# HGRN2 factors of both directions in one tile, the queries read in place, and the second pair of heads projected earlier

## The chip, the core and the metric

The kernel runs on one core of a Trainium2 chip. The metric is the device time of one execution in microseconds (us), as the median of several runs. The engines are named as in the profile: PE (TensorE, matrix products; its weight loads are PEld), DVE (VectorE), ACT (ScalarE), POOL (GpSimd) and SP, whose queue starts nearly all transfers. Each engine works its instructions in order and waits where a semaphore tells it to.

## What is computed

One inference step of a backbone of two layers on 384 tokens (128 of a prompt, 256 of a sample) of width 1024. The first layer's mixer joins windowed attention (mixer A) with a bidirectional HGRN2 of four heads of 128 channels (mixer B), both fed by one input projection. The change is in mixer B alone:

```
qb = silu(q) * dk**-0.5                       # per head, 384 tokens x 128 channels
f  = lb + (1 - lb) * sigmoid(z)               # one gate per direction; log f is the decay, k = 1 - f
cum = cumsum(log f)                           # in chunks
attn[t, s] = sum_k qb[t, k] * exp(cum[t, k] - cum[s, k]) * k[s, k]   for s <= t
o = attn @ v + (qb * exp(cum)) @ state_at_chunk_start
# the backward direction is the same on the flipped sequence; o_f + flip(o_b)
```

The sum over the channels holds a decay that depends on both tokens, so it isn't one matrix product. It is split by halves: for a query t and a key s that lie in the two halves of one block, the decay is a product of one factor up to the border and one from the border.

## The kernel before

The four heads are done as two pairs (pair 0 and pair 1). For a pair, a tile holds 2 heads x 384 tokens = 768 columns, with the 128 channels on the partitions. `hg_proj` projects the queries (`proj_fm` with `ev_q`) and the gates of both directions (`ev_f`): of the gates come f, in two tiles of tag "qf", and 1 - f, in two tiles of tag "X", through a sigmoid on ACT and three steps on DVE each. Every `proj_fm` takes two weight tiles of 512 KB through `wload`: a transfer on SP's queue, a cast on ACT (L122) and a subtraction on DVE (L123); three matmuls of 384 columns for each product, since a float32 is split into a high and a low part.

`hg_levels` then goes through a diagonal step and seven levels. At level lv a block has two halves of m = 2**lv tokens. There are four tiles of factors: forward and backward queries Fq, Bq, and forward and backward keys Fk, Bk. A level does this: four copies on ACT (L890 to L893) put the second halves of Fq and the first halves of Bq into one tile Qc, and the first halves of Fk and the second halves of Bk into one tile Kc. Four multiplies on DVE (L900, 384 columns each) bring the factors to the next level, two small ones (L907, L908) the products over blocks. PE computes six 128 x 128 score matmuls of Kc and Qc ("hs", L872), four and then two, both into the one PSUM bank "lv"; DVE merges each part under a mask into the attention matrix "at" (L911), so the second part waits for the first merge. The two multiplies of the keys and the two of the queries may run as soon as the copies have read the factors.

`hg_out` transposes the keys ("tk", L933), updates the states ("up", L938), multiplies the attention with the values ("ho"), normalises, gates and transposes back ("ty", L971) for the output projection ("o", L127 to L129).

The order of each engine is fixed when the program is built, by a scheduler that simulates the program and takes instructions by priority. Priority follows the order in which the code is written, shifted by `ahead(part)` and the number for that part in the table AHEAD (L30); "lv0" is -30 and "lv1" 0. In the code the order is: context loads `a_ctx`, the key and value projection and the query projection of mixer A, the levels of pair 0, the projection of pair 1, the projections of values ("ib") and output gates ("gb"), the levels of pair 1, the attention, then the two outputs. Beside all that, PE also works off pieces of later conditioning vectors ("ada_acc", L203, "ada_t", L221), which wait for transfers of their own ("ar", L232).

Of the kernel before, what the change touches and what calls it, by code (L numbers as in the profile page):

```python
# [9 lines left out]
F32 = mybir.dt.float32  # L10
# [31 lines left out]
def tile_backbone_step(ctx, tc, I, O):  # L42
# [775 lines left out]
    def mixer_ab():  # L818
# [4 lines left out]
        M = Slots(es, {"one": (1, 0), "pr": (4, 768), "pt": (6, 512), "qS": (2, 1536), "qf": (3, 768),  # L823
                       "X": (8, 768), "at": (2, 768), "vB": (2, 768), "kq": (3, 768), "t2": (5, 512),
# [4 lines left out]
        def hg_tiles():  # L829
            return M.tile("qf", F32), [M.tile("X", F32) for _ in range(4)], [M.tile("qf", F32) for _ in range(2)]  # L830
# [9 lines left out]
        def ev_f(pr, d, X, f):  # L840
            def ev(j, acc):
                c = slice(4 * d + 2 * pr + j, 4 * d + 2 * pr + j + 1)
                sl = slice(j * NTOK, (j + 1) * NTOK)
                sg = M.sm.tile([P, NTOK], F32, tag="sg", name="sg")
                nc.scalar.activation(sg, acc, AF.Sigmoid)
                nc.vector.tensor_scalar(out=X[2 + d][:, sl], in0=sg, scalar1=C["nomlb"][:, c],
                                        scalar2=C["omlb"][:, c], op0=ALU.mult, op1=ALU.add)
                nc.vector.tensor_scalar(out=f[d][:, sl], in0=sg, scalar1=C["omlb"][:, c], scalar2=C["lb"][:, c],
                                        op0=ALU.mult, op1=ALU.add)
                nc.vector.tensor_scalar(out=f[d][:, sl], in0=f[d][:, sl], scalar1=1e-30, scalar2=None, op0=ALU.max)  # L850
            return ev

        def hg_proj(pr):
            q, X, f = hg_tiles()
            proj_fm(w, 768 + 256 * pr, ev_q(q))
            proj_fm(w, 1792 + 256 * pr, ev_f(pr, 0, X, f))
            proj_fm(w, 2304 + 256 * pr, ev_f(pr, 1, X, f))
            return q, X, f


        def hg_levels(q, X, f, out):
            Fq, Bq, Fk, Bk = X
            nc.vector.tensor_tensor(out=Fq, in0=q, in1=f[0], op=ALU.mult)
            nc.vector.tensor_tensor(out=Bq, in0=q, in1=f[1], op=ALU.mult)
            AT = M.tile("at", F32).rearrange("p (b t) -> p b t", b=6)

            def scores(Kc, Qc, take):
                for b0, nb in ((0, 4), (4, 2)):
                    pp = lvt("hs").rearrange("p (b t) -> p b t", b=4)
                    for b in range(nb):  # L870
                        bs = slice((b0 + b) * P, (b0 + b + 1) * P)
                        nc.tensor.matmul(pp[:, b, :], Kc[:, bs], Qc[:, bs], start=True, stop=True)  # L872
                    take(pp[:, 0:nb, :], slice(b0, b0 + nb), nb)
# [7 lines left out]
            scores(Kc, q, diag)  # L881
            yield
            Bf, Bb = f
            for lv in range(7):
                m = 1 << lv
                G = 2 * NTOK // (2 * m)
                V = lambda a: a.rearrange("p (g h m) -> p g h m", h=2, m=m)
# [6 lines left out]
                w_ = max(1, m // 2)  # L894
                bf = Bf.rearrange("p (g h w) -> p g h w", h=2, w=w_)[:, :, :, 0]
                bb = Bb.rearrange("p (g h w) -> p g h w", h=2, w=w_)[:, :, :, 0]
                bc = lambda a: a.unsqueeze(2).to_broadcast([P, G, m])
# [3 lines left out]
                if lv == 0:  # L901
                    nB = M.sm.tile([P, 2, NTOK], F32, tag="nB", bufs=1, name="nB")
                    Bf, Bb = nB[:, 0, :], nB[:, 1, :]
                    nf, nb_ = Bf, Bb
                else:
                    nf, nb_ = bf[:, :, 0], bb[:, :, 0]
                nc.vector.tensor_tensor(out=nf, in0=bf[:, :, 0], in1=bf[:, :, 1], op=ALU.mult)  # L907
                nc.vector.tensor_tensor(out=nb_, in0=bb[:, :, 0], in1=bb[:, :, 1], op=ALU.mult)  # L908
# [8 lines left out]
            for d, B in enumerate((Bf, Bb)):  # L917
                nc.vector.tensor_copy(out=eb[:, d, :], in_=B.rearrange("p (g w) -> p g w", w=64)[:, :, 0])
            out.extend((AT, eb))

        def hg_out(pr, X, AT, eb, vB):
            Fq, Bq, Fk, Bk = X
# [85 lines left out]
        st0 = hg_tiles()  # L1008
# [131 lines left out]
        lv0, lv1 = [], []  # L1140
        a_ctx()
# [4 lines left out]
        st1 = hg_proj(1)  # L1146
# [382 lines left out]
```

## Time and profile before

| | |
|---|---|
| median of 3 runs | 1097.33 us (1095.86 to 1098.22) |
| the profiled execution | 1095.94 us |
| its span in the trace | 1094.1 us |
| PE busy | 1036.0 us, 95% of the span |
| DVE, ACT, POOL busy | 660.6, 440.8, 120.0 us |
| mean granted clock of PE | 0.981 |

The profiled execution is one of its own beside the three runs. Its span runs from the first to the last instruction in the trace; what lies around it is the other 1.84 us. A busy share is a mean over stages with different limits, so the prediction reads single stretches. [...] Instruction durations of engines that work in a pipeline overlap a little, so that a row's start and the next row's start tell more than its length. Float32 matmuls show as two records each.

### The profile page before, as it was taken

To read this page: it belongs to the slowest core of one execution; us is meant where nothing else is said; L and a number is where in the kernel's file an instruction comes from. 1 tells how busy PE (TensorE), PEld (TensorE's weight loads), DVE (VectorE), ACT (ScalarE), POOL (GpSimd) and SP (SyncE) were. 2 spreads that over 40 slices of the span, in tenths; PEclk is the share of its full clock that TensorE was granted. 3 is DMA by queue.
4 is the path that set the end of the run, shared out by engine and by line. 5 is a ranking of instruction groups with operands and counts; after the bars stand their busy time and mean duration, and the time that the engine had idled before them with its cause. 6 is when DMAs were issued, how large, how long until landed. Compare 5 with 4: busy or idle time off the path is not lost. (4 is left out here: it accounts for less than half of the span.)

```text
span 1094.1 us, 15881 instructions
## 1 busy us (share of the span) xinstructions
PE 1036.0 (95%) x6105; PEld 870.7 (80%) x6105; DVE 660.6 (60%) x1140; ACT 440.8 (40%) x804; POOL 120.0 (11%) x166
## 2 busy tenths in 40 slices
PE   5999999987999999999999998979899999999996
PEld 4788767555889999897778786666589999998885
DVE  2575855686598458458236875765489464443237
ACT  2365645363253323232223547545254333332231
POOL 0021201101110000000000343213130000000004
PEclk8999999997999999999999999989999999999998
DMA  9874243484047776766655431144126555543431
GB/s 305 258 222 124 86 142 123 140 275 164 23 150 219 249 221 219 232 210 214 237 190 159 152 108 45 35 150 165 47 79 194 151 172 153 159 135 116 135 116 58
DMA packets 114354, 173.13 MB, mean 158 GB/s; under 512 B 9419, under 2 KB 82150, under 8 KB 114278
## 3 DMA queue, kind: packets, MB, share of 16 engines
q1 hardware_dynamic: 113526, 171.78, 50.0%
q8 instruction: 48, 0.79, 0.3%
q10 hardware_dynamic: 752, 0.34, 0.1%
q14 instruction: 28, 0.23, 0.1%
HBM read 167.84 MB, written 4.24 MB: 157 GB/s over the span
## 5 line engine op out<-in xcount | busy, mean ns | idle before, releaser
L123 DVE TENSOR_TENSOR wl<-wr,wh 128x1024 fp32r<-128x1024 f32 (+4 forms) x200 | 235.7, 1182 | 234.9 <-ACT wh L122 232.3
L122 ACT ACTIVATE wh<-wr 128x1024 fp32r<-128x1024 f32 (+4 forms) x200 | 202.4, 1015 | 347.3 <-PE pf L128 124.0
L127 PE MATMUL pf<-hH,wh 128*128 128x384 f32 x688 | 232.7, 338 | 0.0
L129 PE MATMUL pf<-hH,wl 128*128 128x384 f32 x688 | 232.7, 338 | 0.0
L128 PE MATMUL pf<-hL,wh 128*128 128x384 f32 x688 | 232.6, 338 | 0.0
L129 PEld LDWEIGHTS pf<-hH,wl 128*128 128x128 f32 x688 | 129.4, 188 | 3.1 <-issue 3.1
L128 PEld LDWEIGHTS pf<-hL,wh 128*128 128x128 f32 x688 | 129.4, 188 | 2.7 <-issue 2.6
L127 PEld LDWEIGHTS pf<-hH,wh 128*128 128x128 f32 x688 | 129.4, 188 | 2.3 <-issue 2.2
L128 PE MATMUL o<-wl,aH 128*128 128x512 f32 (+1 forms) x280 | 101.2, 361 | 0.7 <-DVE wl L123 0.7
L127 PE MATMUL o<-wh,aH 128*128 128x512 f32 (+1 forms) x280 | 101.3, 362 | 0.4 <-DVE a L1175 0.4
L129 PE MATMUL o<-wh,aL 128*128 128x512 f32 (+1 forms) x280 | 101.0, 361 | 0.0
L129 PE MATMUL pj<-wh,hL 128*128 128x512 f32 (+3 forms) x240 | 89.0, 371 | 2.0 <-POOL hL L344 1.8
L127 PE MATMUL pj<-wh,hH 128*128 128x512 f32 (+3 forms) x240 | 89.2, 377 | 0.3 <-ACT vA L1106 0.2
L261 DVE SCALAR_TENSOR_TENSOR part<-ar,cT,part 128x512 f32<-128x512 f32 x112 | 80.2, 744 | 15.3 <-DMA ar<-in_w_ada 15.2
L128 PE MATMUL pj<-wl,hH 128*128 128x512 f32 (+3 forms) x240 | 89.0, 371 | 0.0
L110 POOL TENSOR_TENSOR ve<-ve,nhalf 128x1 f32<-128x1 f32 x12 | 7.0, 583 | 617.7 <-DVE ve L530 336.1
L127 PEld LDWEIGHTS o<-wh,aH 128*128 128x128 f32 x280 | 52.9, 189 | 10.2 <-issue 1.4
L128 PEld LDWEIGHTS o<-wl,aH 128*128 128x128 f32 x280 | 52.9, 189 | 9.0 <-DVE wl L123 1.0
L129 PEld LDWEIGHTS o<-wh,aL 128*128 128x128 f32 x280 | 52.8, 188 | 9.2 <-issue 1.2
L129 PEld LDWEIGHTS pj<-wh,hL 128*128 128x128 f32 x240 | 45.1, 188 | 12.2 <-POOL hL L344 2.7
L127 PEld LDWEIGHTS pj<-wh,hH 128*128 128x128 f32 x240 | 44.8, 188 | 10.4 <-issue 2.7
L128 PEld LDWEIGHTS pj<-wl,hH 128*128 128x128 f32 x240 | 45.1, 188 | 8.6 <-issue 1.4
(318 smaller groups left out, 1542.7 us busy)
## 6 DMA issues: line engine op xcount, KB each, us to landing
ar<-in_w_ada SPq DMA_DIRECT2D x80, 512.0 KB
wr<-in_w_ffn_down SPq DMA_DIRECT2D x44, 512.0 KB
wr<-in_w_ffn_gate SPq DMA_DIRECT2D x40, 512.0 KB
wr<-in_w_ffn_up SPq DMA_DIRECT2D x40, 512.0 KB
wr<-in_w_in_ab SPq DMA_DIRECT2D x18, 512.0 KB
ar<-in_w_ada SPq DMA_DIRECT2D x32, 256.0 KB
wr<-in_w_out SPq DMA_DIRECT2D x16, 512.0 KB
wr<-in_w_in_ab SPq DMA_DIRECT2D x16, 256.0 KB
```

The costliest lines, as they stand in the source:

```text
L110: nc.gpsimd.tensor_tensor(out=out, in0=v, in1=nhalf[:, :n], op=ALU.pow)
L122: nc.scalar.activation(hi, raw, AF.Copy)
L123: nc.vector.tensor_tensor(out=lo, in0=raw, in1=hi.bitcast(F32), op=ALU.subtract)
L127: nc.tensor.matmul(out, lh, rh, start=start, stop=False)
L128: nc.tensor.matmul(out, lh, rl, start=False, stop=False)
L129: nc.tensor.matmul(out, ll, rh, start=False, stop=stop)
L261: nc.vector.scalar_tensor_tensor(out=dst, in0=raw[:, j], scalar=sc, in1=dst, op0=ALU.mult, op1=ALU.add)
```

## The change

The factors of both directions come to lie in one tile, keys in one and queries in another: K holds forward and backward keys, Q backward and forward queries, each in 2 x 768 columns and some spare ones ("X" is now 4 tiles of 1664 columns). A view `mixed(X, m)` steps from the first half of a block in one direction to the second half in the other, so that one view names all columns that a level needs. f of both directions is one tile of 1536 columns too.

With this a level has one copy on ACT instead of four: the keys, 768 columns, into a contiguous tile. The queries aren't copied; PE reads them through the view, in runs of m neighbouring columns, as the moving operand. On DVE one multiply of 768 columns takes the place of the two for the keys (L916 in the changed kernel), the two for the queries stay (L918, L919), and the products over blocks are one instruction (L925). In the code, the multiplies of the queries now stand behind the level's scores, which read what they overwrite.

The projection of pair 1 moves ahead of the context loads and of mixer A's projections. Its f takes a tile of tag "qS". The levels themselves stand where they stood.

```diff
@@ mixer_ab @@
-        M = Slots(es, {"one": (1, 0), "pr": (4, 768), "pt": (6, 512), "qS": (2, 1536), "qf": (3, 768),
-                       "X": (8, 768), "at": (2, 768), "vB": (2, 768), "kq": (3, 768), "t2": (5, 512),
+        M = Slots(es, {"one": (1, 0), "pr": (4, 768), "pt": (6, 512), "qS": (2, 1536), "f": (1, 1536),
+                       "X": (4, 1664), "at": (2, 768), "vB": (2, 768), "kq": (3, 768), "t2": (5, 512),
                        "gB": (1, 1536)})
+        N2 = 2 * NTOK
+        def half(X, i):
+            return X[:, i * N2:(i + 1) * N2]
+        def mixed(X, m):
+            v = X[:, 0:2 * (N2 + m)].rearrange("p (h r) -> p h r", h=2)[:, :, 0:N2]
+            return v.rearrange("p h (g a i) -> p h g a i", a=2, i=m)[:, :, :, 0, :]
@@ hg_levels @@
-            Fq, Bq, Fk, Bk = X
+            K, Q = X
+            Fk, Bk, Bq, Fq = half(K, 0), half(K, 1), half(Q, 0), half(Q, 1)
...
-                Kc = M.tile("kq", F32)
-                Qc = M.tile("kq", F32)
-                nc.scalar.activation(V(Qc)[:, :, 1, :], V(Fq)[:, :, 1, :], AF.Copy)
-                nc.scalar.activation(V(Qc)[:, :, 0, :], V(Bq)[:, :, 0, :], AF.Copy)
-                nc.scalar.activation(V(Kc)[:, :, 0, :], V(Fk)[:, :, 0, :], AF.Copy)
-                nc.scalar.activation(V(Kc)[:, :, 1, :], V(Bk)[:, :, 1, :], AF.Copy)
...
-                for eng, T, hh, fac in ((nc.vector, Fk, 0, bf[:, :, 1]), (nc.vector, Bk, 1, bb[:, :, 0]),
-                                        (nc.vector, Fq, 1, bf[:, :, 0]), (nc.vector, Bq, 0, bb[:, :, 1])):
-                    eng.tensor_tensor(out=V(T)[:, :, hh, :], in0=V(T)[:, :, hh, :], in1=bc(fac), op=ALU.mult)
...
-                nc.vector.tensor_tensor(out=nf, in0=bf[:, :, 0], in1=bf[:, :, 1], op=ALU.mult)
-                nc.vector.tensor_tensor(out=nb_, in0=bb[:, :, 0], in1=bb[:, :, 1], op=ALU.mult)
...
-                scores(Kc, Qc, merge)
+                Km, Qm = mixed(K, m), mixed(Q, m)
+                tokens = lambda X: (lambda b: X[:, :, b * gb:(b + 1) * gb, :].rearrange("p h g i -> p g h i"))
...
+                Kc = M.tile("kq", F32)
+                nc.scalar.activation(Kc.rearrange("p (g h i) -> p g h i", h=2, i=m), Km.rearrange("p h g i -> p g h i"),
+                                     AF.Copy)
+                scores(blk(Kc), tokens(Qm), merge)
...
+                nc.vector.tensor_tensor(out=Km, in0=Km, in1=bc(kf), op=ALU.mult)
+                bv = B[:, 0:2 * W].rearrange("p (d g h w) -> p d g h w", d=2, h=2, w=w_)[:, :, :, :, 0]
+                nc.vector.tensor_tensor(out=Qm[:, 1], in0=Qm[:, 1], in1=bc(bv[:, 0, :, 0]), op=ALU.mult)
+                nc.vector.tensor_tensor(out=Qm[:, 0], in0=Qm[:, 0], in1=bc(bv[:, 1, :, 1]), op=ALU.mult)
...
+                nc.vector.tensor_tensor(out=nB, in0=bv[:, :, :, 0], in1=bv[:, :, :, 1], op=ALU.mult)
@@ the order in which the parts are written @@
         lv0, lv1 = [], []
+        st1 = hg_proj(1)
         a_ctx()
         proj_tm(w, 512, 256, evac_kv)
         proj_tm(w, 0, 512, evac_q)
         with ahead("lv0"):
             drain(hg_levels(*st0, lv0))
-        st1 = hg_proj(1)
```

How the orders of the engines move is shown at three places. The first is PE directly behind the output of pair 0 (its last "ho" stands just ahead of these rows). "hs" are the scores of pair 1's levels, "ada_acc" and "ada_t" pieces of the conditioning, "ty" and "o" belong to the output of pair 0, "tk" is the first piece of the output of pair 1. Before:

```order
L203 MATMUL ada_acc<-ar,cT 32x256 x4
L872 MATMUL hs<-kq 128x128 x6
L203 MATMUL ada_acc<-ar,cT 32x256 x4
L872 MATMUL hs<-kq 128x128 x4
L221 MATMUL ada_t<-ident,ada_row 128x128 x2
L872 MATMUL hs<-kq 128x128 x12
L971 MATMUL ty<-ident,kq 128x128 x4
L127 MATMUL o_2428<-wh,hH 128x512
L128 MATMUL o_2428<-wl,hH 128x512
L872 MATMUL hs<-kq 128x128 x2
L971 MATMUL ty<-ident,kq 128x128 x2
L933 MATMUL tk<-ident,X 128x128 x4
```

and in the changed kernel:

```order
L203 MATMUL ada_acc<-ar,cT 32x256 x4
L883 MATMUL hs<-X,kq 128x128 x2
L203 MATMUL ada_acc<-ar,cT 32x256 x4
L883 MATMUL hs<-X,kq 128x128 x4
L221 MATMUL ada_t<-ident,ada_row 128x128 x2
L883 MATMUL hs<-X,kq 128x128 x24
L981 MATMUL ty<-ident,kq 128x128 x2
L883 MATMUL hs<-X,kq 128x128 x2
L981 MATMUL ty<-ident,kq 128x128 x2
L127 MATMUL o_2334<-wh,hH 128x512
```

In the first there are 24 "hs" (four levels of six), in the second 32, and six more follow behind "o", two of the 38 being the end of level 0 and the other 36 the levels 1 to 6. From the "up" that follows on, PE has the same instructions in both kernels; ahead of it there are 800 rows in the first and 788 in the second.

The second place is SP's queue where the first weights of the mixer are fetched, behind the loads of the context keys. "wr" is a weight tile (128x4x256 is one of `proj_fm`, 128x2x256 one of the key and value projection, 128x2x512 one of the query projection), "ar" and "ada_b" are transfers of the conditioning. Before:

```order
L232 DMA ar<-in_w_ada 128x1024
L118 DMA wr<-in_w_in_ab 128x2x256
L232 DMA ar<-in_w_ada 128x1024
L118 DMA wr<-in_w_in_ab 128x2x256
L118 DMA wr<-in_w_in_ab 128x2x512
L197 DMA ada_b<-in_b_ada 32x2x128 x4
L118 DMA wr<-in_w_in_ab 128x2x512 x3
```

and in the changed kernel:

```order
L232 DMA ar<-in_w_ada 128x1024
L118 DMA wr<-in_w_in_ab 128x4x256
L232 DMA ar<-in_w_ada 128x1024
L118 DMA wr<-in_w_in_ab 128x4x256 x2
L197 DMA ada_b<-in_b_ada 32x2x128 x4
L118 DMA wr<-in_w_in_ab 128x4x256
L118 DMA wr<-in_w_in_ab 128x2x256 x4
L118 DMA wr<-in_w_in_ab 128x2x512 x4
```

Four of the six tiles of pair 1's projection now stand in front of those of the key and value projection; two more stand ahead of these rows.

The third place is DVE in one level of pair 1 behind pair 0's output. "X" are the factors, "nB" the products over blocks, "at" the merges, "wl" a weight subtraction for the output projection. Before:

```order
L900 TENSOR_TENSOR X<-X,nB 128x24x16
L908 TENSOR_TENSOR nB<-nB 128x48
L911 COPY_PREDICATED at<-lmask,hs 128x512
L907 TENSOR_TENSOR nB<-nB 128x24
L900 TENSOR_TENSOR X<-X,nB 128x24x16
L911 COPY_PREDICATED at<-lmask,hs 128x256
L123 TENSOR_TENSOR wl<-wr,wh 128x1024
L900 TENSOR_TENSOR X<-X,nB 128x24x16 x2
```

and in the changed kernel, where L905 are the merges, L918 and L919 the multiplies of the queries and L916 that of the keys:

```order
L905 COPY_PREDICATED at<-lmask,hs 128x256
L918 TENSOR_TENSOR X<-X,nB 128x96x4
L919 TENSOR_TENSOR X<-X,nB 128x96x4
L925 TENSOR_TENSOR nB<-nB 128x192
L916 TENSOR_TENSOR X<-X,nB 128x2x48x8
L905 COPY_PREDICATED at<-lmask,hs 128x512
L123 TENSOR_TENSOR wl<-wr,wh 128x1024
L905 COPY_PREDICATED at<-lmask,hs 128x256
```

Before, multiplies of the factors stand on both sides of each merge; now the multiplies of the queries stand only behind the second merge, and a weight subtraction stands between the first merge and the second.

## Rows read from the trace of the kernel before

**Rows 1.** The page, part 1: busy time, share of the span, instructions.
```profile
PE 1036.0 (95%) x6105; PEld 870.7 (80%) x6105; DVE 660.6 (60%) x1140; ACT 440.8 (40%) x804; POOL 120.0 (11%) x166
```

**Rows 2.** Windows: stretch, length; busy PE, PEld, DVE, ACT, POOL; PEclk, DMA, GB/s.
```profile
58.00:205.00 147.00, 146.00 (x813) 108.09 (x811) 94.22 (x187) 77.36 (x153) 24.15 (x28) 1.00 0.45 134
220.00:240.00 20.00, 17.66 (x152) 12.66 (x148) 15.29 (x34) 13.15 (x32) 1.43 (x2) 1.00 0.89 307
240.00:260.00 20.00, 13.73 (x70) 11.13 (x66) 15.13 (x44) 8.03 (x17) 0.69 (x1) 0.74 0.40 124
260.00:280.00 20.00, 16.52 (x70) 12.49 (x71) 9.16 (x22) 5.23 (x18) 2.19 (x3) 0.74 0.47 162
```

**Rows 3.** Timeline of PE, 236:260: start, length, instruction, [idle before, what ended it].
```profile
236.54 1.16 PE L872 MATMUL hs<-kq 128*128 128x128 f32 x8
238.52 0.71 PE L872 MATMUL hs<-kq 128*128 128x128 f32 x4 [0.82 <-DVE at L911]
...
240.31 1.16 PE L872 MATMUL hs<-kq 128*128 128x128 f32 x8 [0.17 <-ACT kq L893]
...
249.59 2.08 PE L872 MATMUL hs<-kq 128*128 128x128 f32 x8 [1.07 <-ACT kq L893]
...
254.92 1.05 PE L872 MATMUL hs<-kq 128*128 128x128 f32 x4
...
256.19 1.06 PE L933 MATMUL tk<-ident,X 128*128 128x128 f32 x4
...
258.14 1.05 PE L938 MATMUL up<-vB,t 128*128 128x128 f32 x8
```

**Rows 4.** Waits, 52:130: engine, line, releaser; us, times, longest.
```profile
PE tk L794 <- ACT sg L845: 0.7, 1, 0.7
```

**Rows 5.** Lines by form, ACT, 58:258: busy us, mean ns; idle before, releasers.
```profile
L122 ACT ACTIVATE wh<-wr 128x1024 fp32r<-128x1024 f32 x27 | 28.4, 1059 | 26.4 <-PE pj L129 13.3 <-DMA wr<-in_w_ffn_up 4.0 <-PE pf L128 3.4
...
L893 ACT ACTIVATE kq<-X 128x384 f32<-128x384 f32 x14 | 7.3, 525 | 0.0
...
L643 ACT ACT_TABLE_LOAD x3 | 3.8, 1283 | 0.1
```

**Rows 6.** Waits, 236:258.
```profile
PE hs L872 <- ACT kq L893: 2.6, 3, 1.4
```

**Rows 7.** Timeline of PE, in the full stretch.
```profile
116.27 1.06 PE L872 MATMUL hs<-kq 128*128 128x128 f32 x8
117.08 0.42 PE L128 MATMUL pf<-hL,wh 128*128 128x384 f32 x1
```

**Rows 8.** Timeline of DVE: the add of 768, and a level of the tail.
```profile
69.62 0.95 DVE L880 TENSOR_TENSOR kq<-X 128x768 f32<-128x768 f32 x1
...
237.74 0.72 DVE L911 COPY_PREDICATED at<-lmask,hs 128x512 f32<-128x512 uint8 x1
...
239.27 0.45 DVE L911 COPY_PREDICATED at<-lmask,hs 128x256 f32<-128x256 uint8 x1 [0.26 <-PE hs L872]
239.61 1.22 DVE L123 TENSOR_TENSOR wl<-wr,wh 128x1024 fp32r<-128x1024 f32 x1
240.74 1.02 DVE L900 TENSOR_TENSOR X<-X,nB 128x384 f32<-128x384 f32 x2
```

**Rows 9.** Windows in the tail and behind it.
```profile
246.00:248.00 2.00, 1.18 (x8) 0.99 (x7) 1.96 (x6) 1.03 (x2) 0.00 (x0) 0.78 0.00 0
258.00:264.00 6.00, 5.31 (x47) 5.06 (x46) 1.52 (x6) 2.69 (x11) 0.70 (x1) 1.00 0.99 353
269.00:277.80 8.80, 7.86 (x18) 5.73 (x19) 3.61 (x9) 0.00 (x0) 0.70 (x1) 0.50 0.38 116
```

**Rows 10.** Timeline of ACT: one copy at level 0, one at level 5.
```profile
67.70 0.58 ACT L890 ACTIVATE kq<-X 128x384 f32<-128x384 f32 x1
...
245.16 0.51 ACT L890 ACTIVATE kq<-X 128x384 f32<-128x384 f32 x1
```

More of the change, by code (lines that the diff above doesn't have):

```diff
@@ L822, in mixer_ab, with hg_tiles @@
         es = ExitStack()
-        M = Slots(es, {"one": (1, 0), "pr": (4, 768), "pt": (6, 512), "qS": (2, 1536), "qf": (3, 768),
-                       "X": (8, 768), "at": (2, 768), "vB": (2, 768), "kq": (3, 768), "t2": (5, 512),
+        M = Slots(es, {"one": (1, 0), "pr": (4, 768), "pt": (6, 512), "qS": (2, 1536), "f": (1, 1536),
+                       "X": (4, 1664), "at": (2, 768), "vB": (2, 768), "kq": (3, 768), "t2": (5, 512),
                        "gB": (1, 1536)})
         gB = M.tile("gB", F32).rearrange("p (a t j v) -> p a t j v", a=2, t=3, j=2)
-        def hg_tiles():
-            return M.tile("qf", F32), [M.tile("X", F32) for _ in range(4)], [M.tile("qf", F32) for _ in range(2)]
+        N2 = 2 * NTOK
[4 more added lines that the diff above has]
+            return v.rearrange("p h (g a i) -> p h g a i", a=2, i=m)[:, :, :, 0, :]
+        def hg_tiles(f):
+            X = [M.tile("X", F32) for _ in range(2)]
+            return half(X[1], 1), X, M.tile(f, F32)
         def ev_q(q):
@@ L861, in hg_levels @@
         def hg_levels(q, X, f, out):
-            Fq, Bq, Fk, Bk = X
-            nc.vector.tensor_tensor(out=Fq, in0=q, in1=f[0], op=ALU.mult)
-            nc.vector.tensor_tensor(out=Bq, in0=q, in1=f[1], op=ALU.mult)
+            K, Q = X
+            Fk, Bk, Bq, Fq = half(K, 0), half(K, 1), half(Q, 0), half(Q, 1)
+            nc.vector.tensor_tensor(out=Bq, in0=q, in1=half(f, 1), op=ALU.mult)
             AT = M.tile("at", F32).rearrange("p (b t) -> p b t", b=6)
@@ L870, in scores @@
                     for b in range(nb):
-                        bs = slice((b0 + b) * P, (b0 + b + 1) * P)
-                        nc.tensor.matmul(pp[:, b, :], Kc[:, bs], Qc[:, bs], start=True, stop=True)
+                        nc.tensor.matmul(pp[:, b, :], Kc(b0 + b), Qc(b0 + b), start=True, stop=True)
                     take(pp[:, 0:nb, :], slice(b0, b0 + nb), nb)
@@ L880, in hg_levels @@
             nc.vector.tensor_tensor(out=Kc, in0=Fk, in1=Bk, op=ALU.add)
[L881 removed]
+            blk = lambda a: (lambda b: a[:, b * P:(b + 1) * P])
+            scores(blk(Kc), blk(q), diag)
+            nc.vector.tensor_tensor(out=Fq, in0=q, in1=half(f, 0), op=ALU.mult)
             yield
[L883 removed]
+            B, W = f, N2
             for lv in range(7):
                 m = 1 << lv
[L886 to L908 removed]
+                G = N2 // (2 * m)
+                gb = G // 6
+                Km, Qm = mixed(K, m), mixed(Q, m)
+                tokens = lambda X: (lambda b: X[:, :, b * gb:(b + 1) * gb, :].rearrange("p h g i -> p g h i"))
                 def merge(pp, bl, nb):
@@ L1006, in x_turn @@
                     nc.scalar.activation(xT[k // 2][:, k % 2, :], tp[:, :NTOK], AF.Copy)
-        st0 = hg_tiles()
+        st0 = hg_tiles("f")
         acc0 = {}
```

21 lines of the change are left out of this document (14 added, 7 removed).

## The prediction

> **What bounds the kernel now.** I read the page's busy times first: TensorE (PE) is busy for 95% of the span [rows 1], so an edit counts only where PE waits or where its clock falls. The windows by stage come next [rows 2]. From the end of the first projections to 205 us PE is busy for 146.00 of 147.00 us at a granted clock of 1.00; nothing that ACT or DVE saves there can be seen in the time, and PE's order decides only when each piece is done. Between 240 and 280 us PE is busy for 13.73 and 16.52 of 20 us and the granted clock is 0.74. That is the one place which the change can reach: the levels of the second pair of heads, when all other PE work of the mixer has run out, and the output of that pair behind them.
>
> The PE timeline of that place [rows 3] shows the levels as bursts of score matmuls, "hs": 8 records are four float32 matmuls, 4 records two, and the two bursts make one level. Level 3 of pair 1 starts at 236.54 and level 6 at 249.59: three periods in 13.05 us, 4.35 us each. After the last burst (254.92) come the transposes "tk" (256.19) and the state update "up" (258.14). From "up" on, PE, ACT and DVE of the changed kernel have the same instructions in the same order as now, so the whole effect is the shift of that "up", and I cost everything to that point.
>
> **The projection that is moved.** The second pair's projection is 144 matmuls of 384 columns, six weight tiles of 512 KB on SP's queue, six casts on ACT and six subtractions on DVE, and six sigmoids with their 14 DVE steps. It now stands ahead of the context loads, the key/value projection and the query projection, and SP's queue carries its tiles ahead of theirs (second pair of order pieces). PE is full there either way, so moved work costs nothing by itself as long as its weights come. DVE prepares the tiles in turn with the first pair's gates; stepping through its order with the durations of these rows, each tile is ready between 0 and 2 us before PE wants it. I take 0 and keep +1.5 for a late tile. What may go is the one PE wait of this stretch, 0.7 us for a transpose behind a sigmoid [rows 4]; I take -0.5.
>
> ACT gains most in plain time. Of the four copies of a level (14 of each, 525 ns [rows 5]) one of 768 columns is left. A cast of 1024 columns takes 1059 ns [rows 5], one of 384 takes 525, so 768 is some 0.85 us: 56 copies, 29.4 us, go and 14, 11.9 us, come. And six loads of the activation table at 1.28 us [rows 5] go, since sigmoids and exponentials no longer take turns: 7.7 us. Together 25 us of ACT. In the full stretch they are worth nothing; in the tail only where PE waits for a copy, 2.6 us in three waits [rows 6].
>
> **What moves against the change.** The scheduler has placed the other work earlier against the levels, since pair 0's levels can start only behind 25 us more of projections. The first pair of order pieces shows it: behind the first pair's output four levels of pair 1 (3 to 6) are left now, and six (1 to 6) in the changed kernel, with nothing but small pieces between them. PE has 12 matmuls less to do ahead of that point: four take 0.81 us in the full stretch (116.27 to 117.08 [rows 7]), so 12 take 2.4 us, and the first scores of the tail come at 236.5 - 2.4 = 234.1.
>
> **What a level costs then.** Now ACT's copies stand between the factors and the scores: DVE may multiply the factors of the next level while PE still reads the copies, so two levels overlap. Without copies PE reads the queries' tile itself, and DVE may multiply it only when the level's last score matmul has read it, and the next level's scores wait for that multiply. One PSUM bank takes the scores, so that the second burst waits for the first merge. The chain of a level from rows of the tail [rows 3, 8]: first burst to the start of the second merge, 236.54 to 239.27, 2.73 us; that merge occupies DVE for 0.34 (the next starts at 239.61); two query multiplies 1.02; some 0.06 to PE: 4.15 us. The keys' multiply of 768 (0.95 as the add of that size) fits beside the first burst. Behind each first merge a weight subtraction of 1.22 us stands in DVE's order (third pair of order pieces); it ends some 0.2 us after the second burst does [rows 8]. So 4.15 to 4.4 us, and I take 4.4: about the 4.35 of now, without a gain from the lost copies. A second side would be DVE's own work in a level, 0.95 + 1.02 + 0.72 + 0.45 and some 0.2 for the block products, 3.3 us; the order excludes it as long as query multiplies stand behind the second merge, and I keep it for a rival.
>
> **The sum.** Level 1 at 234.1, five periods of 4.4 to level 6: 256.1. The normalising of the first pair's output (six steps of DVE and its gates) now falls between levels 5 and 6 and costs some 2 us there, as it does now between the bursts of level 6 (249.59 to 254.92, 5.3 us, against 2.0 at level 3, with 0.9 of it the clock [rows 3]): 258.1. First burst, merge, second burst, "up": 3.2 us, which gives 261.3 at full clock, where "up" is at 258.14 now: +3.2 us.
>
> Then the clock. The granted clock falls at about 247.5, 13 us after the dense work ended, and the four matmuls of level 6 take 2.08 us where level 3's took 1.16 [rows 3, 9]. [...] Now only level 6 pays; in the changed kernel the sparse stretch begins 2 us sooner and about three of its levels fall behind the drop: two more times 1.3, 2.6 us. Sum: 3.2 + 2.6 - 0.5 = **+5.3 us**. The profiled execution takes 1095.94 us (span 1094.1 and 1.84 around it), 1.39 below the median of the runs, 1097.33. So 1101.2 for an execution like the profiled one and 1102.6 for a median.
>
> **The reading of queries in pieces.** No row shows a moving operand whose columns lie apart. At level 0 neighbouring columns come from two halves of a tile, at level 1 two by two, and so on. The nearest rows: ACT's copies that read with a gap at every element took 0.58 us at level 0 and 0.51 at level 5 [rows 10], 0.07 more. I take no cost, since float32 matmuls are slow per column already; doubled level 0 scores would be 12 times 0.2, 2.4 us, and all 84 doubled, 16.8. Below nothing is excluded, since the columns and passes are the same.
>
> [...]
>
> **The rivals.**
> Forecast: a tail of six levels at 4.2 to 4.6 us, half the levels at the low clock, +2.5 to +9: 1099.8 to 1106.3 with 1102.6 as the likeliest. Chance 0.58.
> *Faster*: the copies were what paced the tail (2.6 us of waits for them [rows 6]), and a level falls to DVE's 3.3 us. Then 234.1 + 16.5 + 2 + 3.2 = 255.8 at full clock, 2.3 before now's 258.14; with the early wait gone -2.8: 1094.5. It decides from a period of 3.8 us downward, where five periods end where now's three do. Against it stands the order on DVE, in which the query multiplies follow the second merge. Chance 0.10.
> *No change*: the tail is longer, but the clock gives it back. Now PE runs densely from 269 to 277.8, busy for 7.86 of 8.80 us, with a clock of 0.50 [rows 9], which is worth half of it, some 4.3. Where the clock falls depends on what PE did before; a shifted pattern can leave the dense part at full speed: 5.3 - 4.3 = +1, 1098.3. Against it: the tail is thinner than now, not denser. Chance 0.18.
> *Slower by much*: the clock stays low from level 1 on to the dense part, so that the transposes, "up" and the outputs of pair 1, which now run at 1.00 between 258 and 264 us [rows 9], run at half as well (some 3 us more), and the query reads cost 1 or 2 us: +9 to +13, 1106.3 to 1110.3. Chance 0.14.
>
> **How the numbers follow.** Likeliest 1102.6. About 0.2% of this time, 2.2 us, is what a measurement of this kernel can tell from no change. Slower by more: the forecast and the last rival, 0.72. Within: 0.18. Faster by more: 0.10. For 8 in 10 the range leaves out the faster case and the far end of the slow one: 1097.3 to 1109.5.
>
> **What would show it.** Right: after the first pair's output, 36 score matmuls in six bursts pairs 4.2 to 5.5 us apart; DVE's query multiplies directly behind each second merge and PE waiting for them, no longer for ACT's copy; "up" at 261 to 266 us; ACT's busy time lower by some 25 us with no effect on the end; granted clock 0.50 from about level 3. Wrong: level periods under 3.8 us, an "up" before 258, a clock of 1.00 from 267 on, or PE waiting for weights between 58 and 100 us. If hs matmuls of the full stretch need more than 0.1 us a record, the reading in pieces has a price.

## The result: 1104.98 us, 0.56% slower

The changed kernel takes 1104.98 us (median of 4 runs, 1103.93 to 1106.63), the kernel before in the same comparison 1097.78 us: a ratio of 1.0056, 95% interval 1.0031 to 1.0081. The forecast was 1102.6 us in a range of 1097.3 to 1109.5. The profiled execution has a span of 1102.1 us, 8.0 more than before.

Its page, part 1 (busy time, share of the span, instructions), answers [rows 1]:

```profile
PE 1039.0 (94%) x6105; PEld 875.4 (79%) x6105; DVE 658.6 (60%) x1110; ACT 422.3 (38%) x756; POOL 118.9 (11%) x166
```

ACT has less to do, as the change wants it, and the kernel is slower. The windows by stage, in the columns of [rows 2]:

```profile
58.00:205.00 147.00, 144.03 (x814) 107.74 (x813) 86.64 (x161) 66.19 (x130) 21.86 (x28) 1.00 0.45 142
...
220.00:240.00 20.00, 17.16 (x129) 13.22 (x128) 12.73 (x27) 8.33 (x21) 1.43 (x2) 0.87 0.77 237
240.00:260.00 20.00, 10.70 (x40) 9.05 (x41) 13.97 (x24) 5.37 (x6) 0.00 (x0) 0.50 0.30 92
260.00:280.00 20.00, 15.72 (x93) 12.80 (x93) 15.61 (x42) 8.55 (x24) 2.19 (x3) 0.84 0.45 151
```

Two places have lost most. Between 58 and 205 us PE idles 2.0 us more than before (146.00 busy then, 144.03 now). And from 240 to 260 us PE is busy for 10.70 of 20 us instead of 13.73, with the granted clock (the share of full speed that the throttle left to PE) at 0.50 for the whole stretch instead of 0.74. The PE timeline of that place, as [rows 3]; "hs" is now on line 883 and "up" on 948:

```profile
234.93 2.08 PE L883 MATMUL hs<-X,kq 128*128 128x128 f32 x8
...
240.59 2.05 PE L883 MATMUL hs<-X,kq 128*128 128x128 f32 x8 [1.54 <-DVE bp L291]
...
247.46 2.04 PE L883 MATMUL hs<-X,kq 128*128 128x128 f32 x8 [2.78 <-DVE X L919]
...
253.48 2.05 PE L883 MATMUL hs<-X,kq 128*128 128x128 f32 x8 [1.94 <-DVE X L919]
...
259.11 2.04 PE L883 MATMUL hs<-X,kq 128*128 128x128 f32 x8 [1.54 <-DVE nB L925]
...
266.08 1.06 PE L883 MATMUL hs<-X,kq 128*128 128x128 f32 x8
...
268.50 1.06 PE L948 MATMUL up<-vB,t 128*128 128x128 f32 x8
```

Six levels stand there, 5.6 to 7.0 us apart, and "up" comes at 268.50 instead of 258.14: 10.4 us later. Of these, 2.4 are back at the end of the span (8.0). Some 1.1 of them come from the clock of the dense part behind: windows of the changed kernel, and then of the one before.

```profile
267.00:277.00 10.00, 7.33 (x60) 6.43 (x59) 6.00 (x20) 5.43 (x15) 1.49 (x2) 1.00 0.66 223
277.00:287.00 10.00, 8.14 (x22) 5.50 (x23) 5.98 (x11) 1.12 (x7) 0.70 (x1) 0.66 0.53 173
```

```profile
257.00:267.00 10.00, 7.71 (x58) 6.69 (x56) 4.18 (x14) 5.80 (x17) 1.49 (x2) 0.98 0.81 290
267.00:278.00 11.00, 9.43 (x22) 6.39 (x22) 5.61 (x11) 0.75 (x4) 0.70 (x1) 0.53 0.32 97
```

The dense part holds 22 matmul records in each; PE is busy with them for 9.43 us at 0.53 before and 8.14 us at 0.66 now. Behind it the shift against the kernel before is 9.3 us instead of 10.4. The other 1.3 us go later, nearly all of them 140 us and more behind "up", where PE has the same work. Between 140 and 344 us behind "up" the profiled executions of the kernels below gain up to 3.2 us on the kernel before or lose up to 1.8, so that part isn't put down to the change.

### The profile page after: what moved, and what is told of

It reads as the page before. It is cut to its first block, busy times and chain, and to the rows that moved or that the text cites. A ratio compares the mean times of both kernels' runs of the same rounds, so it can differ in the third digit from the quotient of the medians.

```text
span 1102.1 us, 15795 instructions
## 1 busy us (share of the span) xinstructions
PE 1039.0 (94%) x6105; PEld 875.4 (79%) x6105; DVE 658.6 (60%) x1110; ACT 422.3 (38%) x756; POOL 118.9 (11%) x166
## 4 chain that ended last, share of the span: by engine, by line
PE 73%; DVE 10%; DMA 8%; issue 3%; ACT 3%; POOL 2%; SPq 1%; DVEq 0%; ACTq 0%; POOLq 0%
PE pf L129 9%; PE pf L127 9%; PE pf L128 9%; PE o L127 7%; PE o L128 7%; PE o L129 7%; DMA ar<-in_w_ada 4%; PE pj L129 4%; PE pj L127 4%; PE pj L128 4%; PE ada_acc L203 3%; DVE wl L123 3%; PE hs L883 2%; PE s L722 2%; DVE part L261 2%
```

## The experiments

Two questions were open: which part of the change costs the time (the place of the work, or the rewritten levels), and what paces a level in the tail (the wait for the multiplies, the clock, or the weight tiles). The expectations name the answers by letters.

All kernels were timed beside the kernel before. "Up" is the start of pair 1's first state update in the profiled execution; from there on PE has the same work in all of them (in 8 and 12 a few matmuls stand in another order), and the last matmuls of the last projection start 731 to 740 us later. So "up" is where an edit is read, and the ratio says whether the time follows. Each "up" is that of one execution: the changed kernel and 3, 6 and 9 have the same PE work up to the first scores, and these start at 90.1 to 91.6 us, so 1.6 us of an "up" can be chance. "hs behind" are the score matmuls in PE's order behind pair 0's last "ho" (26 before: the four levels, and two matmuls that end level 2). The scheduler orders each kernel anew; 5 and 9 keep PE's order of the changed kernel and 10 that of 4, and in the others a ratio is that of the edit with its new order.

| kernel | projection of pair 1 | queries | lv0, lv1 | hs behind | first scores | up | ratio to before (95%) |
|---|---|---|---|---|---|---|---|
| before | late | 4 copies | -30, 0 | 26 | 72.9 | 258.14 | 1 |
| changed | early | in place | -30, 0 | 38 | 90.1 | 268.50 | 1.0056 (1.0031 to 1.0081) |
| 1 | early | 4 copies | -30, 0 | 32 | 92.0 | 268.18 | 1.0095 (1.0069 to 1.0121) |
| 2 | late | in place | -30, 0 | 24 | 71.5 | 262.36 | 1.0040 (1.0024 to 1.0056) |
| 3 | early | copied | -30, 0 | 30 | 91.5 | 267.96 | 1.0085 (1.0065 to 1.0105) |
| 4 | early | in place | 300, 100 | 2 | 73.4 | 251.57 | 0.9952 (0.9930 to 0.9974) |
| 5 (changed, mask on POOL) | early | in place | -30, 0 | 38 | 88.2 | 266.88 | 1.0038 (1.0017 to 1.0059) |
| 6 (changed, filled tail) | early | in place | -30, 0 | 38, and 30 of fill | 91.2 | 272.16 | 1.0075 (1.0052 to 1.0099) |
| 7 | late | copied | -30, 0 | 26 | 70.9 | 258.90 | 0.9979 (0.9958 to 1.0000) |
| 8 (before, levels early) | late | 4 copies | 300, 100 | 12 | 72.8 | 248.47 | 0.9891 (0.9865 to 0.9918) |
| 9 (changed, subtraction on POOL) | early | in place | -30, 0 | 38 | 91.6 | 270.86 | 1.0099 (1.0077 to 1.0120) |
| 10 (4, mask on POOL) | early | in place | 300, 100 | 2 | 71.4 | 248.87 | 0.9936 (0.9918 to 0.9955) |
| 11 | late | copied | 300, 100 | 8 | 70.3 | 240.87 | 0.9868 (0.9846 to 0.9889) |
| 12 | late | in place | 300, 100 | 8 | 71.5 | 248.69 | 0.9938 (0.9917 to 0.9959) |

### One part of the change alone: the move (1) and the levels (2)

Kernel 1:

```diff
+        st1 = hg_proj(1)
         a_ctx()
...
             drain(hg_levels(*st0, lv0))
-        st1 = hg_proj(1)
```

Left out here are the tiles that pair 1 needs for it, and that its Fq is multiplied in the queries' own tile, behind the diagonal step.

> The kernel before with only the projection of pair 1 moved to the front; the levels keep their four copies and their separate tiles (pair 1's queries lie in the tile that becomes Fq, and its two f in one spare tile, so that both pairs fit). Behind the output of pair 0 stand 32 score matmuls; before has 26 and the changed kernel 38. Theory A (the place of the levels: what counts is how many levels stand behind the dense work): the up of pair 1 comes some 6 us after the 258.14 us of before (one level of 4.2 and the 2 us by which PE waits at the start of the moved projection), and the time is 1102 to 1103.5 us. Theory B (the rewritten levels are slower by themselves, the move is harmless): only the 2 us of the start show, 1099 to 1100 us.

Kernel 2 is the changed kernel with these two lines the other way round.

> The changed kernel with the projection of pair 1 back at its old place; the levels are the rewritten ones. Behind the output of pair 0 stand 24 score matmuls, where before has 26. Theory A: as before within the measurement, 1095 to 1098.5 us, the up of pair 1 at 256 to 259 us, the start of the first projections without the 3 us wait. Theory B: each level of the tail needs over 5 us where before needs 4.35, and four of them make it 1102 to 1104 us.

Kernel 1 has 1105.57 us against 1096.19 of before, more than theory A gave; kernel 2 has 1100.40 against 1096.19, between the two theories. The move alone brings the whole loss, and the two losses don't add up: 0.95% and 0.40%, with 0.56% for the change. The timeline of kernel 1, whose levels still have their four copies (the releaser "ACT kq" is one of them), shows that the old levels are held in that place too:

```profile
244.47 2.07 PE L877 MATMUL hs<-kq 128*128 128x128 f32 x8 [1.38 <-ACT kq L900]
...
250.48 2.08 PE L877 MATMUL hs<-kq 128*128 128x128 f32 x8 [1.90 <-ACT kq L900]
...
256.55 2.07 PE L877 MATMUL hs<-kq 128*128 128x128 f32 x8 [1.59 <-ACT kq L900]
...
268.18 1.07 PE L945 MATMUL up<-vB,t 128*128 128x128 f32 x8
```

The periods are 6.0 and 6.1 us, as in the changed kernel; ahead of the bursts at 250.48 and 256.55 the cast of a weight tile stands in front of the copies on ACT. The next period, from 256.55 to 261.73, is 5.2 us. But theory A was too simple: with six "hs" fewer behind the output of pair 0, "up" is no earlier. What the two kernels share is the start of the chain. All sixteen steps of the two pairs (a diagonal and seven levels each) go through one PSUM bank, one after the other, and the table's first scores tell when the chain begins. PE timelines of before, of the changed kernel and of kernel 1:

```profile
72.93 1.05 PE L872 MATMUL hs<-qf,kq 128*128 128x128 f32 x8
```

```profile
90.07 0.38 PE L883 MATMUL hs<-X,kq 128*128 128x128 f32 x2
```

```profile
91.99 0.38 PE L877 MATMUL hs<-qf,kq 128*128 128x128 f32 x2
```

The moved projection stands in front of pair 0's first scores, though they don't need it. The chain begins 17 and 19 us later and ends 10 us later. That it ends later because it begins later is argued; no run moves the start alone.

Kernel 2 begins at 71.5 as before does, and is still 4.2 us late at "up". So the levels of the change go on more slowly, in the order that they have there. Its tail, from the PE timeline:

```profile
238.44 1.13 PE L883 MATMUL hs<-X,kq 128*128 128x128 f32 x8 [1.10 <-DVE modT L223]
...
242.93 1.13 PE L883 MATMUL hs<-X,kq 128*128 128x128 f32 x8 [1.54 <-DVE X L919]
...
248.68 2.04 PE L883 MATMUL hs<-X,kq 128*128 128x128 f32 x8 [1.54 <-DVE nB L925]
...
252.96 1.22 PE L883 MATMUL hs<-X,kq 128*128 128x128 f32 x4 [2.23 <-DVE at L905]
...
257.20 1.91 PE L883 MATMUL hs<-X,kq 128*128 128x128 f32 x8
```

The first period, at a clock of 1.00, is 4.49 us, the prediction's 4.4; the last is 8.5. There DVE had a weight subtraction and four normalising steps ahead of the first merge (252.19, hence the 2.23 us that PE waits), and three more gate steps between the merges.

### The levels early (4)

```diff
-"lv0": -30, "lv1": 0
+"lv0": 300, "lv1": 100
```

> The changed kernel with two numbers of the table changed: lv0 from -30 to 300 and lv1 from 0 to 100, so that the scheduler takes the levels earlier. All instructions are the same. Behind the output of pair 0 stand 2 score matmuls instead of 38. Theory A: the tail is gone, PE stays busy and at a clock of 1.00 until the output of pair 1; PE idles some 9 us and loses some 4 us to the clock between 234 and 258 us in before, so 1086 to 1092 us, under both kernels. Theory B: the levels cost DVE and PE their time wherever they stand: not under 1097 us.

1090.88 us against 1096.19: faster than both kernels, in theory A's range at its slow end. The chain begins at 73.4 and "up" comes at 251.57, 16.9 us ahead of the changed kernel, with no instruction added or removed. The two numbers move the start of the chain and also every later turn of it, so this run doesn't part the two. What is left in front of "up" is the output of pair 0: its normalising and gates end the wait there.

### The queries copied again, at both places (3 and 7)

```diff
+                Qc = M.tile("kq", F32)
+                nc.scalar.activation(Qc.rearrange("p (g h i) -> p g h i", h=2, i=m), Qm.rearrange("p h g i -> p g h i"),
+                                     AF.Copy)
-                scores(blk(Kc), tokens(Qm), merge)
+                scores(blk(Kc), blk(Qc), merge)
```

> The changed kernel with a second copy in each level, of the queries into a contiguous tile, as before; the multiplies of the queries may then run while PE still reads. Behind the output of pair 0 stand 30 score matmuls. Theory A: the tail is longer than before's by two thirds of a level, with the 2 us of the start 1100.5 to 1103 us; level 0 takes 1.06 us for four score matmuls instead of 1.49. Theory C (the wait of the query multiplies for the last scores of a level is what makes the levels of the changed kernel long): the period of a level falls from 5.6 to 6.9 us to under 4.9 us at the lower clock, and the time to 1098 to 1100 us.

> The kernel of the second experiment (rewritten levels, projection of pair 1 at its old place) with the queries copied into a contiguous tile again. Behind the output of pair 0 stand 26 score matmuls as in before. Theory C (in the rewritten levels the multiplies of the queries wait for the last scores, so that gates and weight subtractions on DVE add to the chain): the 4 us by which the second experiment is over before are gone, 1095 to 1098 us, the up of pair 1 at 257 to 260 us instead of 262.4. If the loss of the second experiment is only the order that the scheduler happens to take on DVE, it stays: 1099 to 1102 us.

At the old place (7) the copy takes the loss away: 1095.98 us where before has 1098.75, against a ratio of 1.0040 without the copy. Theory C holds there. At the new place (3) it helps nothing, 1105.67 us, and the numbers of both theories were wrong: the chain begins at 91.5 and two of its levels are held. Its last two periods, which nothing holds, are 5.07 and 5.10 us at a clock of 0.50, where the changed kernel's are 5.63 and 5.66: the copy makes a level shorter, by less than theory C gave. DVE timeline of kernel 3, where the second merge stands behind a weight subtraction that waits for its cast:

```profile
240.13 0.72 DVE L905 COPY_PREDICATED at<-lmask,hs 128x512 f32<-128x512 uint8 x1
243.04 1.23 DVE L123 TENSOR_TENSOR wl<-wr,wh 128x1024 fp32r<-128x1024 f32 x1 [2.19 <-ACT wh L122]
244.18 0.43 DVE L905 COPY_PREDICATED at<-lmask,hs 128x256 f32<-128x256 uint8 x1
```

### The start (5 and 10)

In the changed kernel the first matmul of the moved projection waits for PSUM banks, which the sigmoids of pair 0 and a DVE step behind each have to empty (the row names the DVE instruction that comes right behind such a step), and ACT stands in front of them with the band mask. PE and then ACT of the changed kernel, and ACT of before:

```profile
61.98 0.41 PE L127 MATMUL pf<-hH,wh 128*128 128x384 f32 x1 [2.98 <-DVE vT L174]
```

```profile
56.00 0.42 ACT L157 ACTIVATE bmaskR<-t 128x256 fp32r<-128x256 f32 x1 [3.41 <-DMA t<-in_k_band]
```

```profile
54.16 0.42 ACT L157 ACTIVATE bmaskR<-t 128x256 fp32r<-128x256 f32 x1 [1.95 <-DMA t<-in_k_band]
```

The mask's transfer stands behind weight tiles on SP's queue. Two of these tiles are now 512 KB instead of 256, and SP starts the mask's transfer at 51.20 us instead of 48.68; that the one brings the other is argued. Kernel 5 converts the mask on POOL:

```diff
-            nc.scalar.activation(C["bmask"], bmask, AF.Copy)
+            nc.gpsimd.tensor_copy(out=C["bmask"], in_=bmask)
```

> The changed kernel with one instruction on another engine: the conversion of the band mask (line 157) on POOL instead of ACT. PE's order and the rest of ACT's are the same as in the changed kernel. In that kernel ACT waits 3.41 us for the band mask's transfer until 56.00 (before: until 54.16), with the first sigmoids behind it; they free the PSUM banks into which PE projects pair 1, and PE idles for 2.98 us until 61.98. Theory D (that chain is the early loss): the idle time of PE falls to under 1.2 us, the up of pair 1 comes 1.5 to 2.5 us before 268.5, and the time is 1102 to 1104 us. Theory E (the weights or their subtraction are late there): PE still idles 2.5 to 3 us, 1104.5 to 1106 us.

1103.19 us, a ratio of 1.0038 where the changed kernel has 1.0056, and PE starts 1.8 us earlier:

```profile
60.15 0.42 PE L127 MATMUL pf<-hH,wh 128*128 128x384 f32 x1 [1.14 <-DVE vT L174]
```

Theory D holds; "up" is 1.6 us earlier, which one execution alone wouldn't show. The idle time of PE there does: 2.4 to 3.1 us in the six kernels with the early projection and the mask on ACT, and 1.1 and 0.5 in kernels 5 and 10. The intervals of the two ratios overlap, so the trace carries this and not the times.

> The changed kernel with both edits that helped it so far: lv0 300 and lv1 100, and the band mask converted on POOL. Theory D: the start no longer waits, 2 to 3 us under the fourth experiment (1090.9 against 1096.2 of before, a ratio of 0.995): a ratio of 0.991 to 0.994 to before. If the start is hidden by something else here, 0.995 as in the fourth.

With the levels early it is 1088.28 us and 0.9936, "up" 2.7 us ahead of kernel 4: as expected, again with overlapping intervals.

### The clock and the weight tiles (6 and 9)

Kernel 6 fills the wait behind each second burst of pair 1's levels 1 to 5 (`fill` is 6 there and 0 elsewhere; its passing on is left out here):

```diff
+                    if nb == 2:
+                        for i in range(fill):
+                            nc.tensor.matmul(pp[:, 2 + i % 2, :], Kc(i % 6), Kc(i % 6), start=True, stop=True)
```

> The changed kernel with six more score matmuls behind the second burst of pair 1's levels 1 to 5; their result lies in a part of the bank that nothing reads. They fall into time in which PE waits for the merge and the multiplies of the queries, some 1.3 us at full clock. Theory G (the lower clock is what makes the levels of the changed kernel longer than the 4.15 to 4.4 us of the prediction): the granted clock stays at 1.00 through the tail, the periods are 4.1 to 4.9 us, the up of pair 1 comes at 260 to 264 us instead of 268.5, and the time is 1097 to 1101 us although PE does more. Theory F (the weight tiles that come every 6 us, their cast and the subtraction that stands on DVE ahead of a merge pace the levels): the periods stay at 5.5 to 7 us whatever the clock, 1104 to 1107 us.

1108.12 us, slower than either theory gave. Neither holds alone: windows and PE timeline of kernel 6.

```profile
232.00:252.00 20.00, 12.42 (x73) 9.95 (x72) 12.66 (x26) 5.59 (x9) 0.71 (x1) 0.80 0.53 170
254.00:270.00 16.00, 11.88 (x83) 10.11 (x83) 12.88 (x30) 3.79 (x6) 0.70 (x1) 1.00 0.10 33
```

```profile
247.90 1.23 PE L883 MATMUL hs<-X,kq 128*128 128x128 f32 x4 [3.60 <-DVE at L908]
...
258.30 1.13 PE L883 MATMUL hs<-X,kq 128*128 128x128 f32 x8
260.24 0.71 PE L883 MATMUL hs<-X,kq 128*128 128x128 f32 x4 [0.82 <-DVE at L908]
261.49 1.60 PE L887 MATMUL hs<-kq 128*128 128x128 f32 x12 [0.53 <-DVE at L908]
263.19 1.13 PE L883 MATMUL hs<-X,kq 128*128 128x128 f32 x8
```

From 254 to 270 the granted clock is 1.00, where the changed kernel has 0.50 until 265. The period from 258.30 to 263.19 is 4.89 us; its multiplies of the queries ended at 262.26, and the fill holds the next burst for 0.9 us more, so the chain itself is 4.0 us at 1.00. At 0.50 the changed kernel's undisturbed periods are 5.66 and 5.63. But before 254 a subtraction that waited 3.63 us for its cast, and the cast 7.66 us for its tile, held a merge and PE for 3.60 us, and that level alone took 10.2 us. The clock's share of a level, 1.6 us, is worked out from these periods; the bursts alone account for 1.4 of it (2.05 and 1.22 us at 0.50, 1.13 and 0.71 at 1.00). That it can be had back is not shown.

Kernel 9 takes the subtractions of three tiles off DVE:

```diff
-                    pload(0)
-                    pload(1)
+                    early = nc.gpsimd if l == 0 else None
+                    pload(0, eng=early)
+                    pload(1, eng=early)
...
-                            pload(2)
+                            pload(2, eng=early)
```

`wload` hands `eng` on to its subtraction.

> The changed kernel with the weight subtractions of the first three tiles of the feed-forward network on POOL instead of DVE. On DVE two subtractions (at 244.82 and 250.84 in the changed kernel) leave the order of the tail, and nothing else moves there. Theory F (these subtractions wait for a cast that waits for a transfer, and hold the merges that stand behind them): the periods of 6.9 and 6.0 us behind 240.59 become 5.5, the up of pair 1 comes 1.5 to 2.5 us before 268.5, and the time is 1102.5 to 1104 us. If the merges would have been as late without them, the up stays at 268 to 269 us.

1105.92 us and 1.0099: not better. (Of the 2.4 us by which "up" is later than in the changed kernel, 1.4 are there before the tail's first level, where the edit has changed nothing, and 1.0 come in the levels.) The merges came free, but the multiply behind each did not. DVE and then POOL of kernel 9:

```profile
245.81 0.45 DVE L906 COPY_PREDICATED at<-lmask,hs 128x256 f32<-128x256 uint8 x1 [1.31 <-PE hs L884]
246.15 2.10 DVE L919 TENSOR_TENSOR X<-X,nB 128x384 f32<-128x384 f32 x1
248.17 0.55 DVE L920 TENSOR_TENSOR X<-X,nB 128x384 f32<-128x384 f32 x1
```

```profile
245.49 2.35 POOL L123 TENSOR_TENSOR wl<-wr,wh 128x1024 fp32r<-128x1024 f32 x1 [12.24 <-ACT wh L122]
```

A multiply of 0.55 us takes 2.10 while POOL subtracts, 1.55 more than its own time, and the same again at 253.33 (2.14). Without that the periods of 7.18 and 7.21 us would be 5.6, which is what theory F expected; it is worked out, not run.

### Where the levels are early, with the projection late (8, 11 and 12)

> The kernel before with the two numbers of the table as in the fourth experiment (lv0 300, lv1 100). Behind the output of pair 0 stand 12 score matmuls instead of 26. Theory A (the number of levels behind the dense work is what counts): two levels and a third fewer than before at 4 us or so, the up of pair 1 at 248 to 251 us, 1087 to 1092 us, as fast as the fourth experiment. If the early place helps only the changed kernel, 1095 us or more.

> The rewritten levels with the queries copied and the projection of pair 1 at its old place (1096 us), and lv0 300, lv1 100 on top. Behind the output of pair 0 stand 8 score matmuls. Theory A: as the kernel before with early levels, a ratio to before of 0.987 to 0.991. If the rewritten levels cost anything by themselves where they are hidden: 0.993 or more.

> The same without the copy of the queries: PE reads them in place; 8 score matmuls behind the output of pair 0. Theory C (reading in place costs where the levels stand open, as the multiplies then wait for the last scores): hidden behind other work it costs only level 0's slower reading, 12 times 0.11 us or 1.3 us: a ratio to before 0.001 above that of the copied variant, 0.988 to 0.992. If the reading in place costs PE time in all levels, 0.995 or more.

The two numbers alone make the kernel before faster, 1087.00 us against 1098.75 (8). With the rewritten levels and a copy of the queries, which is kernel 7 with the two numbers, it has the lowest ratio, 1080.60 against 1096.34 (11), though its interval and that of 8 overlap; without the copy, kernel 2 with the two numbers, 1088.64 (12), slower than theory C allowed: 0.007 above the copied variant, not 0.001. "Up" is 7.8 us later in 12 than in 11, with first scores 1.2 us later and a clock of 1.00 in both up to "up". So reading in place costs also where the levels are interleaved with other PE work. The likely reason, which no run measured apart, is that each level then passes DVE once more before PE may go on, so that the chain is longer. The last level of kernel 12 shows such a wait, on its PE timeline; kernel 11 has none:

```profile
242.12 1.13 PE L883 MATMUL hs<-X,kq 128*128 128x128 f32 x8 [1.54 <-DVE X L919]
```

The windows from 40 us to "up" of 11 and 12 show PE idle for 3.0 and 5.1 us:

```profile
40.00:240.87 200.87, 197.90 (x1279) 151.30 (x1277) 139.74 (x280) 119.67 (x211) 31.54 (x37) 1.00 0.50 159
```

```profile
40.00:248.69 208.69, 203.58 (x1281) 153.39 (x1279) 139.82 (x279) 105.70 (x195) 31.03 (x37) 1.00 0.48 153
```

2.1 of the 7.8 us are idle time, most of it that wait; 2.0 are longer scores (27.7 us in 11, 29.7 in 12), of which the reading at level 0, below, is some 1.3. The rest is busy time of PE spread over many lines, partly of work that crosses 40 us, and stays open.

## Why the prediction was right, and where its sum was not

- **Signs and luck.** The time lies in the range, but three signs that the prediction gave for being right failed: the levels are 5.6 to 7.0 us apart (4.2 to 5.5), "up" is at 268.50 (261 to 266), and the clock is low from level 1 on (from about 3). The forecast of "up", +5.3 us, is half of the 10.4 measured; that 2.4 us came back behind "up", 1.3 of them late in the run, is luck that brings the time closer to 1102.6.
- **PE bound, one place open.** Right for the levels, and wrong for the start (next point): less of ACT was worth nothing. The instructions of the copies went from 29.5 to 12.7 us (11.9 forecast) and the table loads from 16 to 10. But the four copies of a level overlap on ACT (in level 3 of the kernel before each takes 0.51 us and starts some 0.41 us behind the one ahead of it), so its busy time fell by 18.5 us (440.8 to 422.3), not by 25.
- **The moved projection.** Wrong: forecast -0.5 us with +1.5 for a late tile, measured 2.0 us more of idle PE. I stepped through DVE with the weights, and left out what stands behind them on SP's queue: the mask, ACT's conversion in order, and the sigmoids that free the banks (kernel 5).
- **Levels in the tail.** Right: six instead of four, the first scores at 234.93 (234.1 forecast). The reason given was too narrow: the count alone doesn't set "up" (kernel 1 has six "hs" fewer there and the same "up"). The chain's start, 17 us later, is the likely reason; its turns count as well, as kernel 8, with the first scores of the kernel before, has its "up" 9.7 us earlier.
- **Price of a level.** Right at full clock: 4.4 forecast, 4.49 in kernel 2 and 4.0, worked out, in kernel 6. The waits stand where the text put them, on DVE's multiply (2.78 and 1.94 us at L919).
- **The clock.** The mis-sized term. The sum set a tail at full clock against the 258.14 of before, which holds one slow level already, and then added 1.3 us for two levels, 2.6. The 1.3 us for a level at 0.50 is an estimate from [rows 3], where the first burst takes 2.08 against 1.16 us and the second 1.05 against 0.71; the bursts of the changed kernel and of kernel 6 show 1.4, their periods 1.6. The prediction let the clock fall 13 us after the dense work ended, as in the kernel before. In the changed kernel the last "ho" starts at 231.08, and the clock is down from the first level on, 3.5 us later; windows:

```profile
231.10:234.50 3.40, 1.91 (x19) 0.99 (x21) 1.53 (x4) 1.04 (x5) 0.71 (x1) 1.00 0.82 255
234.50:265.00 30.50, 19.41 (x78) 15.70 (x71) 23.49 (x48) 8.69 (x11) 0.70 (x1) 0.50 0.32 98
```

  So it was at 0.50 for five levels, 1 to 5: 6.5 us by the same price, 3.9 more. That is the mechanism of the rival "slower by much", without its last step: "up" and what follows ran at 1.00.
- **Held merges.** Missing in the sum. I let the subtraction end 0.2 us behind the second burst, because it had its data before [rows 8]. In the changed kernel it waits for the cast, and that for the tile. DVE and ACT of the second level:

```profile
242.67 0.72 DVE L905 COPY_PREDICATED at<-lmask,hs 128x512 f32<-128x512 uint8 x1 [0.69 <-PE hs L883]
244.82 1.23 DVE L123 TENSOR_TENSOR wl<-wr,wh 128x1024 fp32r<-128x1024 f32 x1 [1.42 <-ACT wh L122]
245.96 0.43 DVE L905 COPY_PREDICATED at<-lmask,hs 128x256 f32<-128x256 uint8 x1
```

```profile
243.73 1.06 ACT L122 ACTIVATE wh<-wr 128x1024 fp32r<-128x1024 f32 x1 [7.53 <-DMA wr<-in_w_ffn_up]
```

  The second burst had ended at 244.7, so the merge is 1.3 us late, and 0.4 in the next level.
- **The sum.** "Up" was forecast 5.3 us later and came 10.4 later. The 5.1 us that were missing: 1.3 at the first scores of the tail (233.6 with the 0.5 that was to go, 234.93 measured), 3.9 for the clock and 1.7 for held merges, less 1.0 that remains for levels whose chain was shorter than 4.4 and a normalising that cost less than 2, and less 0.8 from level 6's first burst to "up" (2.4 us, 3.2 forecast). By kernel 6's prices, 1.6 for the clock and 4.0 for the chain, the shares differ and the sum comes out 0.2 lower. Against it 2.4 us came back behind "up", where I had left the clock as it was, and the time moved by 7.2 us. Of that giving back 1.1 us are the mechanism of the rival "no change" (4.3), at a quarter of its size. The start, 2.5 us worse than forecast, shows with 1.3 at the tail; where the rest went stays open.
- **Reading in pieces.** Forecast at no cost, as the score matmuls are slow per column: four of 128 columns take 0.81 us [rows 7], where the projection's matmuls of 384 columns start 0.17 to 0.18 us apart (from 62.23 on in the changed kernel). It has a cost, at level 0 alone. PE timeline of the changed kernel, level 6 of pair 0 and level 0 of pair 1:

```profile
210.78 1.06 PE L883 MATMUL hs<-X,kq 128*128 128x128 f32 x8
...
228.30 1.49 PE L883 MATMUL hs<-X,kq 128*128 128x128 f32 x8
```

  Four score matmuls take 1.49 us at level 0 and 1.06 at level 6, 40% more, both at a clock of 1.00. With the queries copied (kernel 3) level 0 of pair 0 takes 1.05 us, where the changed kernel has 1.49, so it is the reading; what makes it slower at level 0, no run shows. PE timelines of kernel 3 and of the changed kernel:

```profile
117.67 1.05 PE L883 MATMUL hs<-kq 128*128 128x128 f32 x8
```

```profile
116.28 1.49 PE L883 MATMUL hs<-X,kq 128*128 128x128 f32 x8
```

  At 0.50 level 1 (234.93) and level 2 (240.59) are nearly alike, 2.08 and 2.05. Twelve matmuls at 0.11 us are 1.3 us, within the bound of 2.4.

- **The rival "faster".** Excluded by the period: 5.6 us and more, and some 4.0 at full clock, not 3.3.

## What to carry to other kernels

When a long chain of small dependent steps runs beside dense work, ask when it starts and what gives its next step a turn: here two numbers of a priority table were worth 11 to 12 us in four kernels, and the rewrite that saved 18.5 us of busy time on an engine that wasn't the bottleneck cost time. Before taking a copy away, see whether it lets the next step begin while the last is still read (here the ratio to before is 1.0040 without the copy and 0.9979 with it, kernels 2 and 7). A step that is moved can shift what stands behind it on its queues, small loads too (here the start of the mask's transfer, from 48.68 to 51.20 us).

## What the hardware showed that was not expected

DVE's multiply of two tiles took longer while POOL subtracted two tiles: 2.10 and 2.14 us instead of 0.55, so 1.55 and 1.59 us lost, and it ended each time some 0.4 us behind POOL's end (247.84 and 248.25 in kernel 9), while a merge that reads scores from PSUM took its usual 0.45 us beside it. Why the one is held and the other isn't, no run shows.
